# Start addresses of matmul operands in a hybrid decoder layer: every such tile on a multiple of 512 bytes

## The chip, the core and the metric

The kernel runs on one core of a Trainium2 chip. The core has TensorE (PE, matrix products; its weight loads are shown as PEld), VectorE (DVE), ScalarE (ACT), GpSimd (POOL) and SyncE (SP), and 16 DMA engines between HBM and the on-chip memory SBUF (128 partitions, a tile takes so many bytes of each). Matmuls write to PSUM. The metric is device time in microseconds, the median of the runs.

## What is computed

One decoder layer on 512 tokens of width 1024, all in float32: a SwiGLU feed-forward (2816 wide), a token mixer, and a second feed-forward, each with a residual and a layer norm.

```python
x = layer_norm(A * x + 0.5 * swiglu(x, ffn1...))          # silu(x@wg) * (x@wu) @ wd
proj = h @ w_in                                           # q, k, v, z, xbc, dt, two gates
y_attn = sliding_window_sink_attention(q, k, v, sinks) @ w_attn_branch   # 16 heads, 4 kv heads, window 128
y_ssm  = ssd_branch(z, xbc, dt, ...) @ w_ssm_branch       # conv4 + silu, chunked scan of 32 heads, gated rms norm
x = layer_norm(A * x + (sigmoid(ga) * y_attn + sigmoid(gs) * y_ssm) @ w_out)
x = layer_norm(A * x + 0.5 * swiglu(x, ffn2...))
```

The attention's softmax has one extra logit per head, the sink: 16 numbers, broadcast to all partitions.

## The kernel before

Products are taken in float32r with operands split in two parts: `split_w` and `split_act` write a rounded high part and the rest as low part, and `mm3` (lines 120 to 123) issues three matmuls for each product: high x high (L121), and two with one low part (L122, L123). Each loads 128 x 128 weights and streams up to 512 columns. So nearly all of the program is a stream of triples on PE.

There are two kinds of product. `gemm_T` keeps a 128-column weight tile (`wh`, `wl`) as the stationary operand and streams the activations `xT`, `aT` or `uT` (transposed, 512 tokens); one tile is 8 x 3 = 24 matmuls. `down` and `z_tiles` keep 128 tokens of `hT` or `xT` as the stationary operand and stream 512 columns of `wh`, `wl`. The weights come by SP's DMA queue into `raw` (three buffers), ACT casts the high part, DVE subtracts for the low part.

`xT` holds the layer's current activations in both parts, 32 KB a partition, and is the input of both gate/up stages, of every projection of `w_in` and, after the merge, of the output projection. `hT` is the feed-forward's hidden state, `aT` the attention's output, `uT` the ssd branch's.

The order: ffn 1 (gate/up, then `down`, layer norm and transposes into `xT`), V and dt, then the mixer, where `weave` sets steps of the attention or of the ssd scan between projection tiles, then the output projection, and ffn 2. The Tile framework orders instructions and sets semaphores; pools hand out SBUF addresses one tile after the other, so that a tile's start address follows from the sizes of those allocated ahead of it. In the built program the constants end at byte 20608, `mhalf` takes 16 bytes there (32 with rounding), and all later addresses carry that offset:

| tile (operand of matmuls) | start mod 512, before | after |
|---|---|---|
| `ident`, `upper`, `lower`, `lower_r`, `ones` | 128 | 0 |
| `xT` | 160 | 0 |
| `wh`, `wl` (shared buffers) | 64 | 0 |
| `wh`, `wl` (own buffers of a tail of `down`) | 320 | 0 |
| `hT`, `aT`, `uT`, `qT`, `kT`, `xdt`, `seg`, `ud`, `pr` | 64 | 0 |
| `vs` | 64 (some slices 320) | 0 (256) |
| `pt` | 352 | 0 |
| `BT`, `CT`, `Bn` | 64 or 128 | 0 |

The small tiles that cause it: `mhalf` (16 bytes), `cols` (480), `heads` (384), `sinkB` (64), `st` (48) and `mv` (16) in `down`, `sml` (80) in the attention, `rs` (8) in ssd.

Of the kernel before, what the change touches and what calls it, by code (L numbers as in the profile page):

```python
# [9 lines left out]
F32 = mybir.dt.float32  # L10
# [4 lines left out]
P = 128  # L15
# [9 lines left out]
NH = 32  # L25
# [14 lines left out]
def hybrid_layer(  # L40
# [5 lines left out]
    nc = tc.nc  # L46
# [17 lines left out]

    # ---------------------------------------------------------------- constants
    ident = keep.tile([P, P], F32, name="ident")
# [14 lines left out]
    nc.gpsimd.affine_select(band[:, 1], band[:, 1], [[-1, P]], ALU.is_ge, MASKED, base=0, channel_multiplier=1)  # L81
    mhalf = keep.tile([P, 4], F32, name="mhalf")
    nc.vector.memset(mhalf, -0.5)
# [7 lines left out]

    # ---------------------------------------------------------------- helpers
    def split_w(raw, n, shape, pool=None, own=0):
# [31 lines left out]
    def gemm_T(w, act, kk, col=0, ps=None, tok=slice(0, SEQ)):  # L125
        """out^T [128 columns, tokens] of a stationary weight tile."""
        ps = ps or acc()
        wh, wl = w
        n = len(kk)
        for i, k in enumerate(kk):  # L130
            mm3(ps[:, tok], wh[:, i, col:col + P], wl[:, i, col:col + P], act[:, k, 0, tok], act[:, k, 1, tok], i == 0, i == n - 1)
        return ps
# [6 lines left out]
    def split_act(dst, ps):  # L139
        """dst [.., 2, ..] <- the parts of ps."""  # L140
        a = nc.scalar.copy(dst[0], ps)
        b = nc.vector.tensor_tensor(dst[1], ps, f(dst[0]), ALU.subtract)
        return a.ins, b.ins

    def to_xT(t, b, r):
        """natural [128 tokens, 512 of the columns] -> parts of its transpose in xT."""
        ps = sm()
        for j in range(4):
            nc.tensor.transpose(ps[:, j * P:(j + 1) * P], r[:, j * P:(j + 1) * P], ident)  # L149
        d = xT[:, 4 * b:4 * b + 4]  # L150
        split_act((d[:, :, 0, t * P:(t + 1) * P], d[:, :, 1, t * P:(t + 1) * P]), ps.rearrange("p (j t) -> p j t", j=4))

    def norm_scale(pool, st, eps):
        mv = pool.tile([P, 4], F32, name="mv", bufs=2)
        nc.vector.bn_aggr(mv[:, 0:2], st)  # L155
        nc.vector.tensor_scalar_add(mv[:, 2:3], mv[:, 1:2], eps)  # L156
        nc.gpsimd.tensor_tensor(mv[:, 3:4], mv[:, 2:3], mhalf[:, 0:1], ALU.pow)  # L157
        return mv[:, 0:1], mv[:, 3:4]

    def down(act, w, n_k, tail, own, scale, res, pool, gB, bB, eps, then):  # L160
        """natural output of stationary activations, residual and layer norm."""
        pss = [[None] * NT, [None] * NT]
# [9 lines left out]
        tw = pool  # L172
        rs = []
        for t in range(NT):
            r = pool.tile([P, DM], F32, name="r", bufs=4)
            nc.gpsimd.dma_start(r, res[t * P:(t + 1) * P, :])
            rs.append((r, pool.tile([P, 2, 6], F32, name="st", bufs=4)))

# [18 lines left out]
        for t in range(NT):  # L197
            for i, w2 in enumerate(ws):
                mms(1, n2 - tail + i, w2, t)
            residual(1, t)  # L200
            r, st = rs[t]
            mu, rstd = norm_scale(pool, st, eps)
            for half in range(2):
                hs = slice(half * 512, half * 512 + 512)
                nc.vector.scalar_tensor_tensor(r[:, hs], r[:, hs], mu, gB[:, hs], ALU.subtract, ALU.mult)  # L205
                nc.vector.scalar_tensor_tensor(r[:, hs], r[:, hs], rstd, bB[:, hs], ALU.mult, ALU.add)  # L206
                then(t, half, r[:, hs])

    def ffn(wg, wu, wd, g, b, res, then, early=0, first=(), aside=None):
        with tc.tile_pool(name="ffn", bufs=1) as pool:  # L210
# [12 lines left out]
            for i in range(NFF):  # L223
                if early and i == 0:
                    # the tokens whose inputs are ready first
                    for j in range(1):
                        gate_up(j, slice(0, early * P))
                gate_up(i, slice(early * P, SEQ) if early and i < 1 else slice(0, SEQ))
                pg, pu = (ps for _, ps in pairs.pop(i))
                t = pool.tile([P, SEQ], F32, tag="t", name="t", bufs=3)  # L230
                ins = nc.scalar.activation(t, pg, AF.Tanh, scale=0.5).ins
                if aside and i == 4:
                    aside(pool, ins)
                nc.vector.scalar_tensor_tensor(t, t, 1.0, pg, ALU.add, ALU.mult)
                nc.vector.tensor_tensor(t, t, pu, ALU.mult)  # L235
                split_act((hT[:, i, 0], hT[:, i, 1]), t)
            down(hT, wd, NFF, 4, 1, 0.25 / ALPHA, res, pool, gB, bB, LN_EPS / ALPHA ** 2, then)

    # ---------------------------------------------------------------- ffn 1
    nc.scalar.activation(mhalf[:, 1:2], mhalf[:, 0:1], AF.Tanh)  # L240
# [15 lines left out]

    # ---------------------------------------------------------------- small operands
    cols = keep.tile([P, 120], F32, name="cols")
    heads = keep.tile([P, 3, NH], F32, name="heads")
    dtB, aB, dB = (heads[:, i] for i in range(3))  # L260
    sinkB = keep.tile([P, 16], F32, name="sinkB")

    def small_operands(pool, ins):
        """per-channel vectors as columns, per-head vectors on all partitions."""
        rows = pool.tile([P, 2, P], F32, tag="t", name="rows", bufs=3)
        nc.gpsimd.dma_start(rows[:96, 0], conv_w[0].rearrange("w (t p) -> (w t) p", p=P))
        nc.gpsimd.dma_start(rows[:24, 1], conv_b[0].rearrange("(t p) -> t p", p=P))
        for t, v in ((dtB, dt_bias), (aB, a_log), (dB, d_skip), (sinkB, sinks)):
            nc.gpsimd.dma_start(t, v[0].partition_broadcast(P))
        ps = sm()  # L270
        nc.tensor.transpose(ps[:, :96], rows[:96, 0], ident[:96, :96])
        nc.tensor.transpose(ps[:, 96:120], rows[:24, 1], ident[:24, :24])
        with tc.issue_after(ins):
            nc.scalar.copy(cols, ps[:, :120])
            nc.scalar.activation(aB, aB, AF.Exp)
            nc.scalar.mul(aB, aB, -2.0)
            nc.scalar.mul(dB, dB, 0.5)
# [8 lines left out]

    # ---------------------------------------------------------------- mixer
    with tc.tile_pool(name="mix", bufs=1) as mix:
        dtv = mix.tile([P, NT, NH], F32, name="dtv")

        # ------------------------------------------------------------ ssd inputs
        cst = {}

        def conv_tile(tl, pool):
            """one tile of 128 channels through the convolution and twice its silu."""
            w = load_w(wcols(w_in, 0, 8, OFF_XBC + tl * P, P))
# [33 lines left out]
        def z_tiles(g, pool):  # L330
            """twice silu of z, natural, for the group's columns."""
            pss = []
# [24 lines left out]
        def weave(mains, side=(), steps=0, first=0, free=0):  # L357
            """the side's steps spread over the main tiles; a tile's own late part follows the next tile."""
            side, done, late = iter(side), 0, []
# [16 lines left out]

        # ------------------------------------------------------------ attention
        with tc.tile_pool(name="attn", bufs=1) as ap:
            vs = ap.tile([P, NT, 2, 256], F32R, name="vs")
            # V and dt, natural  # L380
            kparts = [(0, 3), (3, 3), (6, 2)]
# [10 lines left out]

            # softplus, decays
            dth = mix.tile([P, NT, NH], F32, name="dth")
# [49 lines left out]
            def attention():  # L444
                units = [(g, t) for g in range(NKV) for t in range(NT)]
                st = {}

                def scores(u):
# [4 lines left out]
                    pr = ap.tile([P, 4, 2 * P], F32, name="pr", bufs=2)  # L453
                    sml = ap.tile([P, 5, 4], F32, name="sml", bufs=3)
                    mx, nm, rs, es, rc = (sml[:, i] for i in range(5))
# [85 lines left out]

        # ------------------------------------------------------------ ssd
        with tc.tile_pool(name="ssd", bufs=1) as sp:
            ysum = sp.tile([P, 8, SEQ], F32, name="ysum")

            def ssd(g):
# [53 lines left out]
                def products(c):  # L600
# [24 lines left out]
                    nc.vector.tensor_tensor(yx, yx, cst.pop(("z", g, c)), ALU.mult)  # L625
                    rs = sp.tile([P, 2], F32, name="rs", bufs=2)
                    sq = sp.tile([P, 512], F32, name="yo", bufs=1)
# [65 lines left out]

        # ------------------------------------------------------------ output projection
        with tc.tile_pool(name="proj", bufs=1) as pool:
# [4 lines left out]

    # ---------------------------------------------------------------- ffn 2
    ffn(f2g, f2u, f2d, ln3g, ln3b, x2d, 
# [30 lines left out]
```

## Time and profile before

| | |
|---|---|
| three runs | 1473.44, 1474.23, 1475.95 us; median 1474.23 us |
| profiled execution: span from first to last instruction | 1474.1 us |
| its own time | within the runs' spread of its span; nothing is shown around the span |
| PE busy | 1448.8 us, 98%, 6700 matmuls |
| DVE / ACT / POOL busy | 791.5 / 482.3 / 199.9 us |
| mean granted TensorE clock | 0.996 of 2.4 GHz |

A matmul's duration in the trace runs from its start to its modelled end, and consecutive ones overlap. How fast PE works is therefore read from the distance between the starts of consecutive matmuls, which is called the step here.

### The profile page before, as it was taken

How to read it: one execution, taken by the hardware profiler on the slowest of the kernel's cores; microseconds unless marked ns; L12 is line 12 of the kernel's file. 1: busy time of each engine (PE TensorE's matmuls, PEld its weight loads, DVE VectorE, ACT ScalarE, POOL GpSimd, SP SyncE). 2: the span in 40 equal slices, each digit the busy share in tenths (PEclk: the TensorE clock that was granted, in tenths of full speed). 3: DMA queues.
4: the chain of work that ended last, by engine and by line, in shares of the span. 5: the costliest groups of instructions: out<-in, count | busy, mean ns of one | idle time of the engine just before them, and what ended most of it. 6: DMA issues, size and time to landing. Idle time of an engine off the chain costs nothing. (4 is left out here: it accounts for less than half of the span.)

```text
span 1474.1 us, 17125 instructions
## 1 busy us (share of the span) xinstructions
PE 1448.8 (98%) x6700; PEld 1169.7 (79%) x6700; DVE 791.5 (54%) x1246; ACT 482.3 (33%) x789; POOL 199.9 (14%) x214
## 2 busy tenths in 40 slices
PE   8999999999999999999999999999999999999997
PEld 6888888888877777887787888878888888888885
DVE  4434343233857884348658688686574434333235
ACT  4322222121346775123434334233312222222220
POOL 1000000000000000145334244361110000000001
PEclk9999999999999999999999999999999999999998
DMA  9433333323432223642231322335635233333321
GB/s 258 116 99 87 100 88 98 99 90 101 136 94 58 58 73 108 190 118 71 79 86 58 93 72 72 93 122 165 217 107 182 87 100 88 98 96 90 101 86 58
DMA packets 195633, 154.46 MB, mean 105 GB/s; under 512 B 6532, under 2 KB 169424, under 8 KB 195552
## 3 DMA queue, kind: packets, MB, share of 16 engines
q1 hardware_dynamic: 188608, 130.17, 30.0%
q0 software_dynamic: 6944, 23.19, 5.1%
q8 instruction: 53, 0.87, 0.2%
q14 instruction: 28, 0.23, 0.0%
HBM read 140.76 MB, written 12.58 MB: 104 GB/s over the span
## 5 line engine op out<-in xcount | busy, mean ns | idle before, releaser
L97 DVE TENSOR_TENSOR wl<-raw,wh 128x1024 fp32r<-128x1024 f32 (+1 forms) x233 | 297.6, 1278 | 431.0 <-ACT wh L96 425.5
L96 ACT CAST wh<-raw 128x1024 fp32r<-128x1024 f32 (+1 forms) x233 | 244.1, 1049 | 714.2 <-issue 337.6
L121 PE MATMUL acc<-xT,wh 128*128 128x512 f32 (+2 forms) x1120 | 447.5, 400 | 0.0
L123 PE MATMUL acc<-xT,wl 128*128 128x512 f32 (+2 forms) x1120 | 440.5, 393 | 0.0
L122 PE MATMUL acc<-xT,wh 128*128 128x512 f32 (+2 forms) x1120 | 440.2, 393 | 0.0
L122 PEld LDWEIGHTS acc<-xT,wh 128*128 128x128 f32 x1120 | 210.6, 188 | 50.7 <-issue 2.9
L121 PEld LDWEIGHTS acc<-xT,wh 128*128 128x128 f32 x1120 | 210.7, 188 | 49.8 <-issue 2.6
L123 PEld LDWEIGHTS acc<-xT,wl 128*128 128x128 f32 x1120 | 210.5, 188 | 49.4 <-issue 0.2
L121 PE MATMUL dn<-wh,hT 128*128 128x512 f32 x352 | 137.3, 390 | 0.0
L122 PE MATMUL dn<-wl,hT 128*128 128x512 f32 x352 | 137.1, 390 | 0.0
L123 PE MATMUL dn<-wh,hT 128*128 128x512 f32 x352 | 137.0, 389 | 0.0
L157 POOL TENSOR_TENSOR mv<-mv,mhalf 128x1 f32<-128x1 f32 x12 | 11.5, 959 | 733.8 <-DVE mv L156 733.8
L568 POOL TENSOR_TENSOR ud<-upper,dAr 128x512 fp32r<-128x512 f32 x64 | 87.1, 1390 | 103.7 <-PE sm L580 103.7
L235 DVE TENSOR_TENSOR t<-t,acc 128x512 f32<-128x512 f32 x44 | 30.3, 688 | 118.6 <-PE acc L123 118.3
L121 PEld LDWEIGHTS dn<-wh,hT 128*128 128x128 f32 x352 | 66.1, 188 | 13.8
L123 PEld LDWEIGHTS dn<-wh,hT 128*128 128x128 f32 x352 | 66.1, 188 | 13.7
L122 PEld LDWEIGHTS dn<-wl,hT 128*128 128x128 f32 x352 | 66.1, 188 | 13.5
L121 PE MATMUL z<-wh,xT 128*128 128x512 f32 x128 | 52.4, 409 | 0.0
L123 PE MATMUL z<-wh,xT 128*128 128x512 f32 x128 | 50.7, 396 | 0.0
L122 PE MATMUL z<-wl,xT 128*128 128x512 f32 x128 | 50.7, 396 | 0.0
L121 PE MATMUL acc<-uT,wh 128*128 128x512 f32 x128 | 50.5, 395 | 0.0
L123 PE MATMUL acc<-uT,wl 128*128 128x512 f32 x128 | 49.9, 390 | 0.0
(212 smaller groups left out, 1697.8 us busy)
## 6 DMA issues: line engine op xcount, KB each, us to landing
raw<-in_w_in_dram SPq DMA_DIRECT2D x66, 512.0 KB, 3.9
raw<-in_ffn_w_gate_dram SPq DMA_DIRECT2D x44, 512.0 KB, 3.9
raw<-in_ffn_w_up_dram SPq DMA_DIRECT2D x44, 512.0 KB, 4.0
raw<-in_ffn_w_down_dram SPq DMA_DIRECT2D x44, 512.0 KB, 3.7
raw<-in_w_ssm_branch_dram SPq DMA_DIRECT2D x16, 512.0 KB, 3.5
raw<-in_w_attn_branch_dram SPq DMA_DIRECT2D x8, 512.0 KB, 4.3
raw<-in_w_out_dram SPq DMA_DIRECT2D x8, 512.0 KB, 4.4
r<-in_x_dram SPq DMA_DIRECT2D x8, 256.0 KB, 6.1
```

What stands on the lines that cost most here:

```text
L96: nc.scalar.copy(h[:, :n], raw[:, :n])
L97: nc.vector.tensor_tensor(l[:, :n], raw[:, :n], f(h[:, :n]), ALU.subtract)
L121: nc.tensor.matmul(ps, lh, rh, start=start, stop=False)
L122: nc.tensor.matmul(ps, lh, rl, start=False, stop=False)
L123: cur["mm"] = nc.tensor.matmul(ps, ll, rh, start=False, stop=stop)
L157: nc.gpsimd.tensor_tensor(mv[:, 3:4], mv[:, 2:3], mhalf[:, 0:1], ALU.pow)
L235: nc.vector.tensor_tensor(t, t, pu, ALU.mult)
L568: nc.gpsimd.tensor_tensor(ud[:, i], upper.unsqueeze(1).broadcast_to([P, 4, P]), f(dAr[:, i, c, h0:h0 + 4]).unsqueeze(2).broadcast_to([P, 4 ...
```

## The change

Allocations are moved, padded or joined until each tile that a matmul reads starts on a multiple of 512 bytes; the last two columns of the table above are the start addresses of the two built programs. `heads` goes to the front, ahead of `ident`: its 384 bytes fill up the 128 that the framework's own constants take. `cols` grows to 512 bytes and holds `mhalf` in its last columns. In `down`, the statistics of the four token tiles (`st`, `mv`) share one tile `sts` of 512 bytes; in the attention the three rotating `sml` buffers become slices of one tile `smls`, whose fourth slice holds the sinks; `rs` is padded to 512 bytes. The load of the sinks moves from `small_operands` to the beginning of `attention`. What is computed is the same.

```diff
+    heads = keep.tile([P, 3, NH], F32, name="heads")
+    dtB, aB, dB = (heads[:, i] for i in range(3))
     ident = keep.tile([P, P], F32, name="ident")
...
-    mhalf = keep.tile([P, 4], F32, name="mhalf")
+    cols = keep.tile([P, 128], F32, name="cols")
+    mhalf = cols[:, 120:124]
...
-    def norm_scale(pool, st, eps):
-        mv = pool.tile([P, 4], F32, name="mv", bufs=2)
+    def norm_scale(sts, t, st, eps):
+        mv = sts[:, 64 + 16 * t:80 + 16 * t]
...
+        sts = pool.tile([P, P], F32, name="sts")
         for t in range(NT):
             r = pool.tile([P, DM], F32, name="r", bufs=4)
             nc.gpsimd.dma_start(r, res[t * P:(t + 1) * P, :])
-            rs.append((r, pool.tile([P, 2, 6], F32, name="st", bufs=4)))
+            rs.append((r, sts[:, 16 * t:16 * t + 12].rearrange("p (a b) -> p a b", a=2)))
...
-    cols = keep.tile([P, 120], F32, name="cols")
-    heads = keep.tile([P, 3, NH], F32, name="heads")
-    dtB, aB, dB = (heads[:, i] for i in range(3))
-    sinkB = keep.tile([P, 16], F32, name="sinkB")
...
-        for t, v in ((dtB, dt_bias), (aB, a_log), (dB, d_skip), (sinkB, sinks)):
+        for t, v in ((dtB, dt_bias), (aB, a_log), (dB, d_skip)):
...
             def attention():
                 units = [(g, t) for g in range(NKV) for t in range(NT)]
                 st = {}
+                smls = ap.tile([P, 4, 8, 4], F32, name="smls")
+                sinkB = smls[:, 3].rearrange("p a b -> p (a b)")[:, :16]
+                nc.gpsimd.dma_start(sinkB, sinks[0].partition_broadcast(P))
...
-                    sml = ap.tile([P, 5, 4], F32, name="sml", bufs=3)
+                    s3 = 4 * g + t
+                    sml = smls[:, s3 % 3]
...
-                    rs = sp.tile([P, 2], F32, name="rs", bufs=2)
+                    rs = sp.tile([P, P], F32, name="rs", bufs=2)
```

Of the instructions' order only one thing changes, and on POOL alone: the load of the sinks (`sinkB`, 16 numbers on 128 partitions). Before, it stands at the program's start, behind the other per-head vectors and ahead of the first layer norm's rows:

```order
L269 DMA heads<-in_a_log_dram 128x32
L269 DMA heads<-in_d_skip_dram 128x32
L269 DMA sinkB<-in_sinks_dram 128x16
L136 DMA gB<-in_ln_g_dram 128x1024
L136 DMA bB<-in_ln_b_dram 128x1024
```

Now it stands behind the four power operations of the first layer norm (they write `sts` in place of `mv`) and ahead of the first store of a gate tile:

```order
L267 DMA rows<-in_conv_b_dram 24x128
L160 TENSOR_TENSOR sts<-sts,cols 128x1 x4
L449 DMA smls<-in_sinks_dram 128x16
L526 DMA gad<-ta 128x512 x7
L531 DMA ta<-gad 128x512
```

One issue has moved past the first feed-forward's loads on POOL's queue. The rows of PE, DVE, ACT and SP stand in the same order in both programs, with the same waits between the engines.

## Rows read from the trace of the kernel before

**Rows 1.** The page: the span, PE's and DVE's busy time, the granted clock by slice.
```profile
span 1474.1 us, 17125 instructions
PE 1448.8 (98%) x6700; PEld 1169.7 (79%) x6700; DVE 791.5 (54%) x1246; ACT 482.3 (33%) x789; POOL 199.9 (14%) x214
PEclk9999999999999999999999999999999999999998
```

**Rows 2.** What PE waited for (us in total, times, longest us): the longest three.
```profile
PE sm L252 <- DMA r<-in_x_dram: 7.1, 3, 6.0
PE sm L149 <- DVE r L206: 2.5, 1, 2.5
PE sm L605 <- DVE seg L589: 2.4, 4, 0.9
```

**Rows 3.** Matmul groups by form: count | busy us, mean ns | idle before.
```profile
L121 PE MATMUL acc<-xT,wh 128*128 128x512 f32 x1088 | 437.7, 402 | 0.0
...
L121 PE MATMUL dn<-wh,hT 128*128 128x512 f32 x352 | 137.3, 390 | 0.0
...
L121 PE MATMUL z<-wh,xT 128*128 128x512 f32 x128 | 52.4, 409 | 0.0
...
L121 PE MATMUL acc<-uT,wh 128*128 128x512 f32 x128 | 50.5, 395 | 0.0
...
L121 PE MATMUL dn<-wh,xT 128*128 128x512 f32 x64 | 26.0, 406 | 0.0
...
L121 PE MATMUL acc<-aT,wh 128*128 128x512 f32 x64 | 24.9, 389 | 0.0
```

**Rows 4.** Timeline of PE in ffn 1's gate/up: start us, duration us, instruction.
```profile
119.92 0.39 PE L121 MATMUL acc<-xT,wh 128*128 128x512 f32 x1
...
121.32 0.39 PE L121 MATMUL acc<-xT,wh 128*128 128x512 f32 x1
```

**Rows 5.** Timeline of PE in ffn 1's down projection.
```profile
299.92 0.39 PE L123 MATMUL dn<-wh,hT 128*128 128x512 f32 x1
...
301.28 0.39 PE L123 MATMUL dn<-wh,hT 128*128 128x512 f32 x1
```

**Rows 6.** Timeline of PE in the output projection, the same lines of `down`.
```profile
1071.83 0.39 PE L121 MATMUL dn<-wh,xT 128*128 128x512 f32 x1
...
1073.24 0.40 PE L121 MATMUL dn<-wh,xT 128*128 128x512 f32 x1
```

**Rows 7.** Timeline of PE in the attention's branch product.
```profile
609.97 0.39 PE L123 MATMUL acc<-aT,wl 128*128 128x512 f32 x1
...
611.33 0.39 PE L123 MATMUL acc<-aT,wl 128*128 128x512 f32 x1
```

**Rows 8.** Timeline of PE: 384 columns of `xT` at the start of ffn 2.
```profile
1094.16 0.34 PE L121 MATMUL acc<-xT,wh 128*128 128x384 f32 x1
...
1095.58 0.34 PE L123 MATMUL acc<-xT,wl 128*128 128x384 f32 x1
```

**Rows 9.** Timeline of PE: the ssd scan's `ud` on `lower_r`.
```profile
766.62 0.39 PE L579 MATMUL sm<-ud,lower_r 128*128 128x512 f32 x1
...
767.32 0.39 PE L580 MATMUL sm<-ud,lower_r 128*128 128x512 f32 x1
```

**Rows 10.** Timeline of PE: the attention's values, 64 weight columns.
```profile
460.80 0.39 PE L122 MATMUL sm<-pt,vs 128*64 128x512 f32 x1
...
461.71 0.39 PE L123 MATMUL sm<-pt,vs 128*64 128x512 f32 x1
```

**Rows 11.** Busy us of each engine in a stretch of the attention (count); clock, DMA share.
```profile
440.00:580.00 140.00, 138.72 (x759) 104.70 (x758) 108.72 (x348) 94.81 (x253) 3.33 (x6) 1.00 0.25 69
```

**Rows 12.** The tile `sinkB`: durations ns min/median/max, first and last start us; landing.
```profile
L468 DVE SCALAR_TENSOR_TENSOR sml<-sml,sinkB x16: 143/153/165, 432.1 to 563.3; 128x4 f32<-128x4 f32 x16
...
L269 POOL DMA_DIRECT2D sinkB<-in_sinks_dram x1: 547/547/547, 4.5 to 4.5; - x1
...
DMA to landing us min/median/max: 6.3/6.3/6.3
```

**Rows 13.** Timeline of POOL from the first layer norm on: start, duration, [idle before <-releaser].
```profile
388.85 0.93 POOL L157 TENSOR_TENSOR mv<-mv,mhalf 128x1 f32<-128x1 f32 x1 [7.19 <-DVE mv L156]
535.05 0.61 POOL L522 DMA_DIRECT2D gad<-ta  x1 [145.27 <-ACT Bn L326]
```

More of the change, by code (lines that the diff above doesn't have):

```diff
@@ L201, in down @@
             r, st = rs[t]
-            mu, rstd = norm_scale(pool, st, eps)
+            mu, rstd = norm_scale(sts, t, st, eps)
             for half in range(2):
@@ L273, in small_operands @@
         with tc.issue_after(ins):
-            nc.scalar.copy(cols, ps[:, :120])
+            nc.scalar.copy(cols[:, :120], ps[:, :120])
             nc.scalar.activation(aB, aB, AF.Exp)
```

## The prediction

> **What bounds the kernel now.** I read the page's head first: PE is busy for 1448.8 of 1474.1 us and its granted clock is full in every slice but the first [rows 1]. Then PE's own waits: the longest is the start (7.1 us for x), and behind it nothing is over 2.5 us [rows 2]. So no stage waits for weights, VectorE or ScalarE to a degree that matters, and the time is the number of matmuls times the step from one start to the next. The busy figure does not say how good that step is, because durations overlap: a matmul shows 390 to 409 ns [rows 3] while the next one starts after some 230.
>
> So I took steps from the timeline, in stages with different operands. Ffn 1's gate/up streams `xT` over `wh`/`wl`: six steps from 119.92 to 121.32 us, 233.3 ns each [rows 4]. Ffn 1's down projection, 128x512 as well: 1.36 us for six, 226.7 ns [rows 5]. The output projection goes through the same lines of `down`, with the same weights' path, but with `xT` in place of `hT` as the stationary operand: 1.41 us for six, 235 ns [rows 6], which the rounding of the starts does not tell from 233.3. The attention's branch product goes through the same `gemm_T` as the gate/up stage, with `aT` in place of `xT`: 1.36 us, 226.7 ns [rows 7]. So the extra 6.67 ns follows `xT`, in either role and through either code path; in the gate/up and the down stretch PE has nothing to wait for.
>
> What is different about `xT` is where it starts: 160 past a multiple of 512 (table of addresses), against 64 or 320 for all that it meets. Taken mod 128, `hT`, `aT`, `uT` and all weight tiles start at the same 64; `xT` starts at 32. Two more pairs were looked at for a test. `ud` (64) over `lower_r` (128, so 0 mod 128): three steps in 0.70 us, 233.3 ns [rows 9], the slow step, although both are multiples of 64. And `pt` (96 mod 128) over `vs` (64), with only 64 weight columns: four steps in 0.91 us, 227.5 ns [rows 10], close to the fast one. So what fits best is not that an operand lies badly by itself, but that the two operands of a matmul start at different offsets within 128 bytes; with half the weight columns it costs little.
>
> **The change part by part.**
>
> *Addresses.* After it, all pairs have the same offset, 0. The forecast gives each pair that now differs the step of those that now agree, 226.7 instead of 233.3 ns, 6.67 ns less. Counted: `gemm_T` on `xT` at 512 columns is 3 lines of 1088, 3264; `z_tiles` 3 x 128 = 384; the output projection 3 x 64 = 192; together 3840 [rows 3], which has one line of each three, and 25.6 us. `ud` adds 64, 0.4 us. Shorter products on `xT`: 48 with 384 columns and 96 with 288 (V and dt). The 384-column step is 1.42 us / 8 = 177.5 ns [rows 8], 17.5 over 384 columns at 2.4 GHz (160 ns); at 512 columns (213.3 ns) the slow step is 20.0 over and the fast one 13.4. The excess shrinks with the columns, so the shorter ones may gain less than 6.67 ns; bounds 0 and 144 x 6.67 = 1.0 us, and I take the 1.0. The 48 with 128 columns and `pt` I leave at nothing (84 x 0.8 ns). Sum: 25.6 + 0.4 + 1.0 = 27.0 us.
>
> The gain is not read off at full value everywhere. In the two feed-forwards, 2112 of these matmuls (14.1 us), PE runs through without waits, and the down stage shows that the weight path (512 KB for 24 matmuls, cast and subtraction) keeps up with 226.7 ns. In the mixer (the other 12.9 us) VectorE and ScalarE carry the attention and the scan beside PE: in 440 to 580 us VectorE is busy for 108.7 of 140 us, 78% [rows 11]. With PE faster by 3% that becomes some 80%, still below full, but the few chains that PE waits for already (2.5 us for a layer norm, 2.4 us for `seg` [rows 2]) keep their length while PE arrives earlier. What is given back lies between 0 and 12.9 us; PE waits for little there now, so I take a value near the lower end, 2 us, about as much again as the longest of these waits. What is late next are these same waits.
>
> *The sinks' load.* At the start POOL loses one DMA issue of 0.55 us [rows 12] ahead of rows that the first layer norm reads at some 389 us [rows 13]: no effect (0 to 0.5 us). In the attention the load stands behind the fourth power, which ends at 389.8 us; the next POOL instruction, a gate tile's store, waits 145 us, until 535 us [rows 13]. It also waits until ffn 1's tiles at its address are done, which is the end of that stage. The first reader is VectorE at 432.1 us, and the old load took 6.3 us from issue to landing [rows 12]: issued up to 6 us after the power (an estimate for the rest of that layer norm), it would land by 402, 30 us early. Cost nothing; if that cover were gone, VectorE would stand still for at most the landing, 6.3 us once. Nothing is queued behind it on POOL but the stores that wait until 535 us anyway.
>
> *Shared statistics.* `sts`, `smls` and `rs` hold what separate tiles held; instruction counts stay, and the waits between PE, VectorE, ScalarE and SP are the same in both programs. Had the joined tile added a false wait, it would be for the power on POOL, 0.93 us [rows 13], 12 times in the program, 11 us at most; no such wait is in the order, so I take 0.
>
> Sum: 1474.1 - 27.0 + 2.0 = 1449.1 us, against a span that is 0.1 us below the median of the runs. Forecast **1449 us**, with a range of its own of 1445 (nothing given back, a little more from small fp32 products) to 1454.
>
> **Rivals.**
>
> *Deeper.* The 226.7 ns still lie 13.4 ns over 512 columns at 2.4 GHz, and all agreeing pairs of the trace start at 64 mod 128; a start at 0 mod 512 was never seen with both operands. If that remainder is also a matter of the start, 5620 matmuls with 512 columns (3840, 1632 on `hT`, `uT`, `aT`, 64, 84) lose up to 13.4 ns more, 75 us: 1372 us. Against it: it shrinks with the columns in [rows 8] (17.5 of 160 against 20.0 of 213.3 ns), as something paid along the stream would, not once at a bad start. Chance 0.11. The Trainium skill, "TensorE: Matmul & The Clock Gate", section "Wait — 56ns, not 53.3ns?", states for bf16 that back-to-back matmuls at full clock start N / 2.4 + 2.5 ns apart, 215.7 ns at 512 columns; no matmul of this trace does, and by that figure this rival would end near 1387 us.
>
> *No change.* The slow step follows the place and not the offset: `xT` and `lower_r` are the two matmul operands in the lowest 54 KB, all their partners lie above, and the change leaves both there. The rows on `xT` and `ud` fit this as well; only `pt` over `vs` [rows 10], both high up, slightly over 226.7 ns, speaks against it, by an amount at the limit of the rounding. Then the time stays at 1474 us. Chance 0.14. A rule points the same way: the Trainium skill, "SBUF — State Buffer", section "Door 1: The DMA port swizzle", says that SBUF is read in lines of 16 bytes and that only crossing into a new line costs. Every start address here, 160 included, is a multiple of 16, so by it the change gains nothing; that [rows 5] and [rows 6] differ is then not explained by lines.
>
> *Slower.* A start at 64 mod 128 is good by itself and any other is bad: `xT` (32) is bad, and `lower_r` (0) is bad although its partner stands at 64 [rows 9]. Then the change moves every operand to the bad place: `xT` keeps 233.3 ns and the 1632 fast matmuls on `hT`, `uT` and `aT` [rows 5, 7] go to it, 1632 x 6.67 = 10.9 us, 1485 us. It decides from the first down stage on, where the step would be 233 instead of 227 ns. Nothing in the trace excludes it, since no 512-column pair has both operands at 0; but a place that is good at an odd multiple of 64 and bad at an even one is less likely than a relation between two streams. Chance 0.06.
>
> *The mixer gives its share back.* VectorE's chains set the pace there once PE is quicker, and only the feed-forwards' 14.1 us stay: 1460 us. Speaks for it VectorE's 78%; against it that PE is busy for 138.7 of the 140 us [rows 11]. Chance 0.05.
>
> **How the numbers follow.** Forecast 0.64, no change 0.14, deeper 0.11, slower 0.06, mixer 0.05. The range 1440 to 1476 us takes in the forecast, the mixer's case and no change, about 0.82, and leaves out the deeper and the slower case. A measurement of this kernel tells about 0.2% (3 us) from no change: faster 0.64 + 0.11 + 0.05 = 0.80, same 0.14, slower 0.06.
>
> **What would show it.** In the profile after, 24 matmuls of a gate/up tile take 5.44 instead of 5.60 us; the step of the output projection equals that of the down stages; the steps in the down stages stay at 226.7 ns; PE's waits in the mixer grow by a microsecond or two; `ud` over `lower_r` goes to 226.7 ns; the sinks land near 400 us and no VectorE instruction waits for them. The prediction is wrong if gate/up stays at 233 ns (place, not offset), if the down stages move at all (up: the slower rival, down: the deeper one), or if the steps fall as said and the time does not, which would be the mixer.

## The result, and the profile after

Four runs of the changed kernel gave 1451.72 us (1449.98 to 1453.2), against 1473.84 us (1473.22 to 1475.95) for the kernel before on the same chip: a ratio of 0.9842 [0.9828, 0.9855], 22.1 us less. The profiled execution has a span of 1451.5 us, 22.6 us less than [rows 1]. A span leaves out 1.7 us of a run's time (the profiled execution took 1453.2 us, the longest of the four), so it is compared with spans only.

The head of the page after (span; busy time, share and count of each engine):

```profile
span 1451.5 us, 17121 instructions
PE 1426.5 (98%) x6700; PEld 1169.7 (81%) x6700; DVE 791.5 (55%) x1246; ACT 482.1 (33%) x789; POOL 195.3 (13%) x214
```

PE is busy for 98% again, with the same 6700 matmuls. As before, the share hides the gain; the steps show it. PE's timeline after (start, duration, instruction): gate/up, down, `ud`, output projection.

```profile
119.89 0.39 PE L124 MATMUL acc<-xT,wh 128*128 128x512 f32 x1
...
121.25 0.39 PE L124 MATMUL acc<-xT,wh 128*128 128x512 f32 x1
...
299.87 0.39 PE L126 MATMUL dn<-wh,hT 128*128 128x512 f32 x1
...
301.23 0.39 PE L126 MATMUL dn<-wh,hT 128*128 128x512 f32 x1
...
754.33 0.39 PE L583 MATMUL sm<-ud,lower_r 128*128 128x512 f32 x1
...
755.01 0.39 PE L584 MATMUL sm<-ud,lower_r 128*128 128x512 f32 x1
...
1053.01 0.39 PE L124 MATMUL dn<-wh,xT 128*128 128x512 f32 x1
...
1054.37 0.39 PE L124 MATMUL dn<-wh,xT 128*128 128x512 f32 x1
```

Gate/up: six steps in 1.36 us where [rows 4] has 1.40. The output projection: 1.36 where [rows 6] has 1.41. `ud` over `lower_r`: three in 0.68 where [rows 9] has 0.70. Down stays at 1.36, as in [rows 5]. So the 512-column pairs with different starts came to the step of those with equal starts, and those did not move.

What PE waited for after (us in total, times, longest), the longest two behind the start; `seg` is a tile of the scan that VectorE finishes, `r` the rows of the layer norm:

```profile
PE sm L609 <- DVE seg L593: 2.8, 4, 1.2
PE sm L152 <- DVE r L210: 2.7, 1, 2.7
```

These are the waits of [rows 2], both somewhat longer. By stage, from the starts of the same matmuls in both traces (us; the expected gain is the prediction's 6.67 ns times the stage's matmuls, before anything is given back):

| stage | before | after | gain | expected |
|---|---|---|---|---|
| start, to the first gate/up matmul | 13.80 | 12.03 | 1.77 | 0 |
| ffn 1 gate/up | 248.23 | 240.47 | 7.76 | 7.0 |
| ffn 1 down | 122.99 | 122.92 | 0.07 | 0 |
| V, dt, first projections | 43.22 | 42.63 | 0.59 | 1.4 |
| attention | 160.84 | 159.22 | 1.62 | 3.0 |
| `y_attn` product | 43.56 | 43.52 | 0.04 | 0 |
| ssd scan (with `ud`) | 387.88 | 384.63 | 3.25 | 7.2 |
| ssd branch's product | 21.80 | 21.76 | 0.04 | 0 |
| output projection | 51.85 | 51.16 | 0.69 | 1.3 |
| ffn 2 gate/up | 250.02 | 243.30 | 6.72 | 7.0 |
| ffn 2 down | 119.48 | 119.45 | 0.03 | 0 |

The feed-forwards gave what was forecast and 0.4 us more, of which the start is the reason (below). The mixer, down to the output projection, kept 6.2 of 12.9 us. The start gave 1.8 us that was in no sum.

The sinks after, by tile (durations ns min/median/max, first and last start; landing):

```profile
L449 POOL DMA_DIRECT2D smls<-in_sinks_dram x1: 604/604/604, 385.9 to 385.9; - x1
...
L472 DVE SCALAR_TENSOR_TENSOR smls<-smls x16: 144/154/163, 421.9 to 552.1; 128x4 f32<-128x4 f32 x16
...
DMA to landing us min/median/max: 2.8/2.8/2.8
```

They land near 389 us; the first reader starts at 421.9 and waits for no DMA. 33 us of cover, where some 30 were forecast.

### The profile page after: what moved, and what is told of

It is laid out like the page before. It is cut to its first block, busy times and chain, and to the rows that moved or that the text cites. A ratio compares the mean times of both kernels' runs of the same rounds, so it can differ in the third digit from the quotient of the medians.

```text
span 1451.5 us, 17121 instructions
## 1 busy us (share of the span) xinstructions
PE 1426.5 (98%) x6700; PEld 1169.7 (81%) x6700; DVE 791.5 (55%) x1246; ACT 482.1 (33%) x789; POOL 195.3 (13%) x214
## 5 line engine op out<-in xcount | busy, mean ns | idle before, releaser
L99 ACT CAST wh<-raw 128x1024 fp32r<-128x1024 f32 (+1 forms) x233 | 244.3, 1050 | 694.4 <-issue 323.7
L124 PE MATMUL acc<-xT,wh 128*128 128x512 f32 (+2 forms) x1120 | 441.9, 395 | 0.0
L125 PE MATMUL acc<-xT,wh 128*128 128x512 f32 (+2 forms) x1120 | 434.8, 388 | 0.0
L126 PE MATMUL acc<-xT,wl 128*128 128x512 f32 (+2 forms) x1120 | 433.8, 387 | 0.0
L160 POOL TENSOR_TENSOR sts<-sts,cols 128x1 f32<-128x1 f32 x12 | 11.9, 990 | 719.9 <-DVE sts L159 719.9
```

The source lines that it names most:

```text
L99: nc.scalar.copy(h[:, :n], raw[:, :n])
L124: nc.tensor.matmul(ps, lh, rh, start=start, stop=False)
L125: nc.tensor.matmul(ps, lh, rl, start=False, stop=False)
L126: cur["mm"] = nc.tensor.matmul(ps, ll, rh, start=False, stop=stop)
```

## The experiments

All ratios are against the kernel before on the same chip. Three things were in dispute: whether the two operands' relation or each one's own place counts, what the mixer did with its share, and whether the sinks' load took part.

### e1_xt_only: before, with `xT` alone brought to its partners

```diff
-    mhalf = keep.tile([P, 4], F32, name="mhalf")
+    mhalf = keep.tile([P, 16], F32, name="mhalf")
...
-    sinkB = keep.tile([P, 16], F32, name="sinkB")
+    sinkB = keep.tile([P, 40], F32, name="sinkB")[:, :16]
```

`xT`, `hT`, `aT` and the weight tiles then all start at 192 mod 512, `lower_r` at 128; nothing else of the change is done.

> The kernel before with two tiles made larger and nothing else: mhalf 16 to 64 bytes, sinkB 64 to 160 bytes. xT then starts at 192 past a multiple of 512, as all weight and activation tiles do; nothing but ident and its neighbours (128) is where the change puts it, no tile is at a multiple of 512, statistics and sinks stay as they were. Offset theory (a pair is slow when its two operands start at different offsets within 128 bytes): gate/up step 226.7 ns, time as after the change less only what ud over lower_r gains, 1450 to 1453 us, ratio to before 0.984 to 0.987. Theory that a multiple of 512 is what counts: no operand gains, 1474 us. Theory of place (low addresses): 1474 us. Theory that 64 mod 128 is good by itself: 1452 us too.

Measured: 1454.27 us, 0.9862 [0.9843, 0.9881]. PE's timeline in gate/up:

```profile
119.85 0.39 PE L121 MATMUL acc<-xT,wh 128*128 128x512 f32 x1
...
121.21 0.39 PE L121 MATMUL acc<-xT,wh 128*128 128x512 f32 x1
```

1.36 us for six at 192, far from any multiple of 512, and nearly the whole of the change's gain. 12 numbers of padding in one tile and 24 in another do nearly all that its moves do.

### e2_weights_32: after, with everything behind `xT` moved by 32 bytes

```diff
+    shift = keep.tile([P, 8], F32, name="shift")
+    nc.vector.memset(shift, 0.0)
```

The unused tile stands behind `xT`: `xT`, `ident` and `lower_r` stay at 0, all other operands start at 32.

> The changed kernel with one unused tile of 32 bytes behind xT: xT, ident and lower_r stay at multiples of 512, all weight tiles, hT, aT, uT and the rest start at 32. Offset theory: every matmul that meets xT is slow again (233.3 ns), hT, aT, uT with the weights stay at 226.7 ns; 1470 to 1476 us, ratio to before 0.998 to 1.002. Theory of place: as after the change, 1452 us. Theory that each operand has to be at a multiple of 512: all 512-column matmuls slow, down stages too (233.3 ns), some 1482 us or more.

Measured: 1474.8 us, 0.9999 [0.9989, 1.0008], the whole gain gone. PE's timeline, gate/up and down:

```profile
119.92 0.40 PE L126 MATMUL acc<-xT,wh 128*128 128x512 f32 x1
...
121.32 0.40 PE L126 MATMUL acc<-xT,wh 128*128 128x512 f32 x1
...
299.86 0.39 PE L128 MATMUL dn<-wh,hT 128*128 128x512 f32 x1
...
301.22 0.39 PE L128 MATMUL dn<-wh,hT 128*128 128x512 f32 x1
```

Gate/up is back at 1.40 us although `xT` lies on a multiple of 512; down, where both moved, keeps 1.36. The sinks' new place and the shared statistics are in this kernel too, and bring nothing that its time shows.

### e3_all_32: after, with every tile moved by 32 bytes

```diff
-    heads = keep.tile([P, 3, NH], F32, name="heads")
+    heads = keep.tile([P, 104], F32, name="heads")[:, :96].rearrange("p (a b) -> p a b", a=3)
```

> The changed kernel with heads 32 bytes larger at the front: every tile that a matmul reads starts at 32 past a multiple of 512, all alike. Offset theory: as after the change, gate/up and down both 226.7 ns, 1450 to 1454 us, ratio to before 0.983 to 0.987. Theory that multiples of 512 count, or of 64: every matmul at 233.3 ns or slower, 1482 us or more.

Measured: 1453.8 us, 0.9854 [0.9838, 0.987]. PE's timeline in gate/up:

```profile
120.29 0.39 PE L124 MATMUL acc<-xT,wh 128*128 128x512 f32 x1
...
121.65 0.39 PE L124 MATMUL acc<-xT,wh 128*128 128x512 f32 x1
```

No tile that a matmul reads is on a multiple of 512 and the step is 226.7 ns. With e2 this settles that the relation of the two starts decides here, and not the place of either. How far apart still counts as equal, and how fine a common start may be, the trains below show.

### e4_trains: trains of 25 matmuls on chosen starts

```python
        for i in range(25):
            a = (i % 6) * per + mo // each
            w = sta[1] + (0 if fixed else (i % 8) * 512 // each) + so // each
            nc.tensor.matmul(ps[:m, :n], sta[0][:, w:w + m], mov[0][:, mov[1] + a:mov[1] + a + n], start=i == 0, stop=i == 24)
```

`each` is the bytes of a number, `per` how many make 2048 bytes; `mov` and `sta` are the tile of the moving operand and of the weights, with an offset. A tile's name tells the train: `m32s0n512c128z` has the moving operand at 32 and the weights at 0 past a multiple of 512, 512 columns, 128 weight columns.

> Not the layer: x is loaded and copied into three tiles, and 42 trains of 25 matmuls run back to back, each with its own start of the moving operand (m), of the weights (s), its columns and weight columns, all from the same two tiles; the output is one of the products. Its time says nothing, the steps within each train do. Offset theory: 226.7 ns at 512 columns wherever m and s agree mod 128 (0/0, 16/16, 32/32, 64/64, 96/96, m 128 or 256, s 128), 233.3 ns where they differ (16, 32, 48, 64, 96, 192, 160/64), about 228 to 230 ns with 64 weight columns and 32 apart; low or high tiles make no difference. Theory of multiples of 512: only 0/0 is fast. Theory of place: the trains with a low moving and a high weight tile are slow at 0/0. Open: whether 4 and 8 bytes apart count, whether a repeated weight tile does, and what is left over the 213.3 ns at bfloat16.

PE's timeline, a train to a row; its length less the last matmul's 0.39 us, over 24, is the mean step:

```profile
170.38 4.53 PE L77 MATMUL m0s0n384c128z<-hi 128*128 128x384 f32 x25
174.75 4.50 PE L77 MATMUL m32s0n384c128z<-hi 128*128 128x384 f32 x25
179.08 3.45 PE L77 MATMUL m0s0n288c128z<-hi 128*128 128x288 f32 x25
182.38 3.49 PE L77 MATMUL m32s0n288c128z<-hi 128*128 128x288 f32 x25
...
203.16 5.88 PE L77 MATMUL lowmovz<-lo,hi 128*128 128x512 f32 x25
...
214.54 5.99 PE L77 MATMUL lowmov160s64z<-lo,hi 128*128 128x512 f32 x25
...
237.55 5.57 PE L77 MATMUL bfz<-bf 128*128 128x512 bf16 x25
242.96 5.56 PE L77 MATMUL bf32z<-bf 128*128 128x512 bf16 x25
```

At 384 columns a difference of 32 bytes costs nothing (over their last steps both trains stand at 173.3 ns), at 288 some 1.6 ns a step (3.49 against 3.45 us). A moving operand in low SBUF is slow only when it starts at 160 against 64 (5.99 us; 5.88 at 0 over 0, whose last steps are 226.7 ns). Against the expectation, 128 over 0 takes 5.99 us too, where 0 over 0 takes 5.83, and 16 over 16 takes 5.91: the offset within 128 bytes is not the rule. In bfloat16 there is no difference (both settle at 215.8 ns). A train needs some steps to settle, so these means sit a little over the settled step; hence e10.

### e5_sinks_only: before, with the sinks' load moved and the addresses outside the attention kept

```diff
-    sinkB = keep.tile([P, 16], F32, name="sinkB")
+    space = keep.tile([P, 16], F32, name="space")
+    nc.vector.memset(space, 0.0)
...
+                sinkB = ap.tile([P, 16], F32, name="sinkB")
+                nc.gpsimd.dma_start(sinkB, sinks[0].partition_broadcast(P))
```

The unused tile keeps the addresses up to the attention as they were; inside it, the tiles allocated behind the new `sinkB` lie 64 bytes higher.

> The kernel before with one part of the change: the sinks are loaded into a small tile of the attention at its beginning, and an unused tile of the same size keeps all other addresses in place. The prediction's step (the move costs and brings nothing): time as before within 0.2%, the stretch from the first transpose of x to the first down stage 256 us as before. Rival, from the profile after, where that stretch is 246.8 us and 7.0 us of it are the matmuls' steps: the start is some 2 us shorter without this load, 1472 us, ratio 0.9985 to 0.999.

Measured: 1475.07 us, 0.9995 [0.9986, 1.0004]. The move of the load is worth between +0.6 and -2.1 us and cannot be told from nothing. The start (to the first gate/up matmul 13.43 us, 13.80 before) and gate/up 1 (247.38 us, 248.23 before) are together 1.2 us shorter in the one trace, and the attention is as long as before (204.06 against 204.07 us, with V and dt).

### e6_fill: after, with eight idle matmuls where PE waits for `seg`

```diff
+                    for _ in range({(0, 2): 3, (3, 2): 5}.get((g, c), 0)):
+                        nc.tensor.matmul(py, lower_r, xT[:, 0, 0], start=True, stop=True)
```

They run ahead of the scan's `xdt` product in two of its steps, and their result is overwritten.

> The changed kernel with eight extra matmuls (lower_r with 512 columns of xT, into a PSUM tile that the real product overwrites) at the two places of the scan where PE waited for seg and the clock fell to 1.2 GHz afterwards (group 0 chunk 2: three, group 3 chunk 2: five). Theory of the clock: what the scan stage kept back, about 3 of its 384.6 us, is two stretches of 3.4 us at half clock that follow these waits; with PE busy there they go, scan stage 381 to 382 us as in the kernel with only xT moved, whose profile had no such stretch; time 1448 to 1450 us. Rival (VectorE's chain sets the pace, the clock does not matter): the extra matmuls come on top or leave it, 384 to 386 us, time 1452 to 1454 us.

Ahead of the second place PE waits 1.16 us for `seg` in after. Two stretches of the scan in after, and the slow part of the first (us, then PE, PEld, DVE, ACT, POOL busy and instructions, granted clock, DMA share, GB/s):

```profile
677.00:687.00 10.00, 9.12 (x38) 6.13 (x36) 9.72 (x16) 3.84 (x6) 1.30 (x1) 0.83 0.17 52
965.00:980.00 15.00, 13.84 (x62) 10.19 (x61) 11.87 (x17) 3.90 (x7) 6.20 (x9) 0.89 0.52 163
...
680.10:683.50 3.40, 3.40 (x8) 1.50 (x6) 3.40 (x5) 1.58 (x3) 0.00 (x0) 0.50 0.27 77
```

The same in e6_fill:

```profile
677.00:687.00 10.00, 9.54 (x47) 7.01 (x47) 9.76 (x15) 3.84 (x6) 1.30 (x1) 1.00 0.17 52
965.00:980.00 15.00, 15.00 (x74) 11.79 (x73) 13.44 (x18) 5.24 (x9) 7.15 (x10) 1.00 0.57 174
```

And in e1_xt_only, whose scan begins 3.4 us later, the same places and its waits for `seg`:

```profile
680.40:690.40 10.00, 9.02 (x44) 6.57 (x43) 9.72 (x16) 3.84 (x6) 1.30 (x1) 1.00 0.16 52
968.40:983.40 15.00, 13.80 (x68) 10.91 (x67) 13.43 (x19) 5.26 (x9) 5.59 (x10) 1.00 0.56 174
...
PE sm L605 <- DVE seg L589: 2.9, 4, 1.2
```

In after PE works part of each stretch at 1.2 GHz, the 3.4 us with a granted clock of 0.50 (a mean of 0.83 over 10 us). Before, the scan has no such stretch. With two of them the scan takes 384.6 us (after, e7, e8), with one 382.95 (e3), with none 381.65 (e1) or, with the eight matmuls in it, 382.8 (e6). So a stretch costs about 1.5 us. Timed, e6 gives 1452.2 us, 0.9836 [0.9822, 0.9849], against 0.9845 [0.9831, 0.9858] for after: the interval cannot tell 1.3 us, and the time is one that the expectation gave to the rival. The stretch's price is from traces alone. Nor did the matmuls remove the wait; part of it moved to the next tile, `yx` (0.6 us in after):

```profile
PE sm L644 <- DVE yx L637: 1.8, 1, 1.8
PE sm L611 <- DVE seg L593: 1.1, 2, 0.8
```

The wait by itself does not decide the clock: e1 has the same four waits for `seg`, the longest 1.2 us too, and keeps full clock.

### e7_late: after, with the output projection's first transposes issued later

```diff
...
+                if late and t == 2 and i == 0:
+                    with tc.issue_after(cur["mm"].ins):
+                        for half in range(2):
+                            to_xT(0, half, rs[0][0][:, half * 512:half * 512 + 512])
...
```

PE's longest wait in the projection is for the first token tile's layer norm. Here its transposes are queued behind the third tile's first matmuls.

> The changed kernel, in which the output projection's transposes of the first token tile are queued behind the first matmuls of the third instead of into the second's, so that PE does not wait for the layer norm there. Theory: the wait of 2.7 us and the half-clock stretch behind it go, output projection 51.2 us becomes 47 to 48 us, time 1448 us. Rival: the wait comes back at a later transpose, 51 us, 1452 us.

Measured: 1448.67 us (1447.59 to 1450.65), 0.9816 [0.9803, 0.983], the lowest median of all that ran. The projection takes 48.64 us in place of 51.16. The wait there after, run again on the same chip (e8; 2.7 us in the first trace):

```profile
PE sm L152 <- DVE r L210: 4.2, 1, 4.2
```

and in e7_late:

```profile
PE sm L152 <- DVE r L214: 2.0, 1, 2.0
```

In 1050 to 1072 us the granted clock is 1.00 in e7 and 0.84 in e8 (0.92 in the first trace of after): what the later issue saves is part of the wait and the half clock behind it.

### e8_after_again: the changed kernel beside e5, e6 and e7

> The changed kernel once more on the same chip as the runs beside it, for comparison with them: 1450 to 1453 us, ratio 0.983 to 0.986. If the stretches at half clock in the scan follow from where the waits happen to fall, their number in this profile may differ from two, and the scan stage is 381.6, 383.0 or 384.6 us for none, one or two.

Measured: 1453.74 us (1450.77 to 1455.58), 0.9845 [0.9831, 0.9858], the first ratio again. Between the two traces of the same kernel the output projection alone differs by more than 0.1 us, 53.64 us against 51.16, with the wait for the layer norm at 4.2 against 2.7 us.

### e9_fill_late: e6 and e7 together, three token tiles' transposes late

```diff
...
+                turned = {(2, 0): 0, (3, 0): 1, (3, 3): 2}.get((t, i)) if late else None
+                if turned is not None:
+                    with tc.issue_after(cur["mm"].ins):
...
```

> The changed kernel with both: the eight extra matmuls of the scan, and the output projection's transposes each queued behind later matmuls (the first token tile's behind the first six of the third tile, the second's behind the first six of the fourth, the third's behind the fourth's). Theory: the gains add up, since they lie in different stages: scan 382.8 us, output projection 47.5 to 48.6 us, no stretch at half clock between start and end; time 1446 to 1448 us, ratio to before 0.980 to 0.982. Rival: ffn 2 waits for the transposes that come later, what the projection saves is lost there, 1450 to 1452 us.

Measured: 1449.13 us, 0.9824 [0.9811, 0.9838]: not better than e7, so the gains did not add up as expected. The projection falls to 47.52 us and the scan is at full clock (382.77), but ffn 2's gate/up takes 244.50 us, 1.2 more than after. The trace's waits of PE name the reason, two that are in no other list:

```profile
PE acc L125 <- DVE xT L145: 1.0, 1, 1.0
PE acc L124 <- ACT xT L144: 0.8, 1, 0.8
```

Transposes issued too late reach the next stage's first matmuls: part of the wait was moved, not removed.

### e10_trains_long: trains of 41, each behind 20 matmuls of equal starts

> Not the layer: trains of 41 matmuls of one tile pair, each behind 20 matmuls with both operands at a multiple of 512, so that each starts from the same state; the output is one of the products and the time says nothing. The first trains showed the fast step at equal offsets and at 256 apart, the slow one at 128 and 192 apart, against the theory of 128 bytes. Theory of 256: 256 apart is fast at any place (256/0, 0/256, 64/320), 64, 128, 192, 320, 384 and 448 apart are slow, equal offsets from 32 on are fast and 8/8 and 16/16 are not. Theory of 128, if the first trains were disturbed by what ran ahead of them: 128/0, 384/0 and 0/128 fast too. The train with two breaks of four transposes: if the slow steps after a switch are a state that takes time to fade, some 10 matmuls at 228 to 236 ns follow each break, else 226.7 ns at once.

PE's timeline, a train to a row (length less 0.39 us, over 40, is the step):

```profile
37.36 9.46 PE L75 MATMUL m0s0n512z<-hi 128*128 128x512 f32 x41
...
51.19 9.73 PE L75 MATMUL m32s0n512z<-hi 128*128 128x512 f32 x41
...
65.33 9.56 PE L75 MATMUL m64s0n512z<-hi 128*128 128x512 f32 x41
...
93.42 9.72 PE L75 MATMUL m128s0n512z<-hi 128*128 128x512 f32 x41
...
121.66 9.46 PE L75 MATMUL m256s0n512z<-hi 128*128 128x512 f32 x41
...
233.51 9.72 PE L75 MATMUL m8s8n512z<-hi 128*128 128x512 f32 x41
...
247.63 9.59 PE L75 MATMUL m16s16n512z<-hi 128*128 128x512 f32 x41
...
261.60 9.49 PE L75 MATMUL m32s32n512z<-hi 128*128 128x512 f32 x41
...
289.33 9.50 PE L75 MATMUL m64s320n512z<-hi 128*128 128x512 f32 x41
```

9.46 us is 226.7 ns a step, 9.72 is 233.3. Equal starts are fast, and so are starts 256 apart (256/0; 64/320, whose first steps are slower). 128 apart is slow (128/0, and 384/0, whose train takes 9.72 us too); 64 and 320 over 0 lie between (9.56 us each, 229). Equal starts at 8 are slow and at 16 half-way; at 32 they settle to 226.7 after some ten slower steps, so that their train takes 9.49 and not 9.46 us. The kernel's own pair of before, 160 over 64, takes 9.72 us for the train, its 233.3 a step. One more train, with transposes between its matmuls, was meant to show what an interruption costs; its transposes were scheduled ahead of the whole train, so it shows nothing. Trains with fewer columns: at 448, 32 over 0 takes 206.7 ns a step and 0 over 0 takes 202.7, a difference of 4.0 in place of 6.7.

## Why the prediction was right, point by point

*The relation of the two starts, not the place.* Right in kind: e2 and e3 are as opposite as the same two tiles can make them. Wrong in size: the prediction took the starts mod 128. By e10 it is mod 256, and equal starts have to be multiples of 32. The rows of before with 128 weight columns fit that too: `xT` against its partners is 96 apart, `ud` against `lower_r` 64, and the own weight buffers at 320 against `hT` at 64, which were fast, 256. Since the changed kernel makes every pair equal, or 256 apart in some slices of `vs`, the wrong size did not touch the sum. That is luck: a change that had left pairs 128 apart would have been forecast as fast. Why the relation counts, no run shows.

*27.0 us of steps.* 14.1 us were for the feed-forwards' gate/up; they gave 14.5, of which some 0.7 in ffn 1 belong to the start. `ud` fell as said. The 1.0 us for shorter products was too much: V and dt with 288 columns, 0.64 of it, took 13.62 us in place of 13.66, and in e4 a difference of 32 bytes costs 1.6 ns a step at 288 columns; the 384-column step went from 177 to 174 ns, not by 6.67.

*2 us given back in the mixer.* This is the term that was mis-sized: 6.7 us were. 3.0 are two stretches at half clock in the scan (e1, e3 and e6). Some 2 are steps above the fast one, read as not yet settled: of 1548 matmuls of 512 columns on `xT` between 400 and 1030 us, 350 are between 228.5 and 243 ns, together 2.1 us over 226.7. After, PE's timeline in the attention, behind four transposes of `pr`, shows how:

```profile
445.41 0.39 PE L126 MATMUL acc<-xT,wl 128*128 128x512 f32 x1
...
447.49 0.39 PE L126 MATMUL acc<-xT,wl 128*128 128x512 f32 x1
...
448.85 0.39 PE L126 MATMUL acc<-xT,wl 128*128 128x512 f32 x1
```

Nine steps of 231 ns, and then six of 226.7. In a weave of tiles and small products this comes again and again; that the interruption is the cause is argued from such rows, since the train that was to test it shows nothing. About 0.6 are the V and dt products above, and 0.6 the output projection, where the wait for the layer norm and half clock behind it vary from run to run: 51.16 and 53.64 us in the two traces of after, and 50.48 in e5, whose steps are slow. What is left, some 0.4 us, has no name. VectorE's mean share, by which the prediction weighed this term, did not show what cost it. Where PE waits for `seg`, VectorE is busy for 9.72 of 10.00 us, in after and in e1 alike; yet e1, without the half clock behind the waits, gains 6.2 of the scan's 7.2 us. Nor could the prediction's clock row show such stretches: a 9 in it stands for 90% or more of a slice of 37 us, and the one slice below that is the last and not the first, as the prediction has it [rows 1].

*The sinks and the shared statistics at nothing.* Their cover held, as the rows after show. But the start and ffn 1's gate/up are 2.5 us shorter than the steps explain. Two things at least changed there: the load that left, and the addresses that `x` and the first weights are loaded to, which the prediction did not consider. With the step's 7.0 us added back where it is fast, the two stages take 262.0 and 262.9 us in the two kernels with the old load (before, e1), and 260.6 to 260.8 in the three whose load moved and whose starts are the old ones or 32 bytes off (e5; e2, e3). They take 259.4 to 260.1 us in the five with both changes (after, e6 to e9). In e3 all starts are 32 bytes off and nothing else differs from after; while the last blocks of `x` come in, its DMA engines move less. First e3, then after (us, then PE, PEld, DVE, ACT, POOL busy and instructions, granted clock, DMA share, GB/s):

```profile
10.50:12.00 1.50, 1.50 (x8) 1.12 (x7) 1.25 (x2) 0.74 (x2) 0.00 (x0) 1.00 1.17 291
...
10.50:12.00 1.50, 1.50 (x12) 1.35 (x11) 1.20 (x3) 1.26 (x3) 0.00 (x0) 1.00 1.15 344
```

The first gate/up matmul starts at 13.02 us in e3 and at 12.03 in after. So by the traces, one of each kernel, some half of the 2.5 us is the load's and half the addresses'. The only timed comparison of the load alone, e5, has 0.5 us, between +0.6 and -2.1; e2, with the load moved and the steps slow, has 0.1, between +1.2 and -1.6. So the prediction's bound for the load, 0.5 us, was probably too narrow, and its size stays open.

*The sum.* 25.0 us net were forecast; 22.6 came in the span. 4.7 us more were given back in the mixer, and 2.5 were gained at the start; the rest is rounding and ffn 2's 0.3. The two errors have opposite signs, and that is luck: without the start's 2.5 us the time would have been some 1454 us, the upper end of the forecast's own range.

*The rivals.* No change (the place): refuted by the gate/up step after, fast with `xT` as low as before, by e2, which makes it slow with `xT` left where it is, and by e4's low train, fast at 0 over 0. The Trainium skill, "SBUF — State Buffer", section "Door 1: The DMA port swizzle", has SBUF in 16-byte lines and a penalty for an access that crosses into a new one; 32 over 0 starts both operands on such a line and costs 6.6 ns (e10: 233.3 against 226.7), which lines do not explain, so the measurement decides. Slower (64 good by itself): refuted by the down rows after and by e10's 0 over 0. Deeper: refuted, 0 over 0 stands at 226.7, 13.4 ns over its columns. The Trainium skill, "TensorE: Matmul & The Clock Gate", section "Wait — 56ns, not 53.3ns?", gives 215.7 ns for bf16; e4's bf16 train agrees (215.8 settled), and float32r does not reach it at any start tried. The mixer that gives all back: it gave back half, so the time lies between this rival's 1460 and the forecast, near the forecast.

## What to carry to other kernels

Before an address is tuned, compare the step (start to start) of matmuls of one shape on different operands: a busy share of 98% hid a 3% slower step, and one pair that is fast already shows what to reach. Then give the moving and the stationary operand of full float32r matmuls the same start mod 256, on a multiple of 32; two paddings did that here (e1), and a multiple of 512 for everything was not needed for the steps; only the loads at the start gained by it, some 1 us by the traces of e3 and after. And when PE gets faster, look for the waits that it now reaches earlier and for slices at half clock behind them: moving one token tile's transposes (e7) was worth 0.3% of the kernel.

## What the runs showed of the hardware

- The step of a float32r matmul with 512 columns and 128 weight columns depends on the difference of its operands' starts: 226.7 ns at 0 and 256 bytes, 229 at 64 (moving operand ahead), and 232.4 to 233.7 at 32, 96, 128 and 192 (e10).
- Equal starts must lie on a multiple of 32 bytes (8/8: 233.2, 16/16: 230.0, 32/32: 226.7 settled); weights at 16 under a moving operand at 0 are fast all the same (226.7; all e10).
- With starts 32 apart the loss is smaller for fewer columns: 6.7 ns at 512, 4.0 at 448 (e10), none at 384, where both settle at 173.3, and 1.6 at 288 (e4). bfloat16 shows none at 512 columns (215.8 settled, with equal starts and 32 apart).
- Behind some interruptions, or a change of the pair, some ten matmuls pass before the fast step is reached (after: nine of 231 ns behind four transposes; e10: 64 over 320, 32 over 32); 256 over 0 behind 0 over 0 is fast at once.
- Waits of PE of about 1 us in the scan were followed by stretches at 1.2 GHz in some kernels and not in others with the same waits; what decides was not found (after and e1).
- At the start, the loads of `x` and the first weights moved 327 to 346 GB/s from 10.5 to 12 us into tiles on multiples of 512 bytes (after, e6 to e9), and 291 to 297 into tiles 32 bytes off or at the old starts (e2, e3, e5).
